# A hybrid DeltaNet, gating and Fourier step: first convolution tap on ScalarE, side work spread over the q, k, v loop, output weights' steps at other blocks

## The chip, the cores and the metric

The kernel runs on one core of one Trainium2 chip. The metric is the device time of one execution in microseconds (us); the time of a kernel is the median of several runs. The core has five engines that each work through a queue of their own in a fixed order: TensorE (PE, matrix products into PSUM; PEld is its loading of weights), VectorE (DVE), ScalarE (ACT), GpSimd (POOL) and SyncE (SP), which here only issues DMA transfers. An instruction waits in its queue on semaphores for what it needs from other engines, and everything behind it in that queue waits with it.

## The reference

One layer of a hybrid model is computed for 2048 sample tokens and 128 prompt tokens (2176 in all, width 1024), in float32. Cut to what matters here:

```
shift, scale, gate = split(silu(cond) @ w_ada + b_ada)
xn = rmsnorm(h) * (1 + scale) + shift
qkv, beta, dec, z_a, u_b, v_b, z_b, x_c, z_c, gates = split(xn @ w_in)
qkv = silu(conv3(qkv))                      # three taps along the tokens, per channel
q, k, v = split(qkv);  q, k = l2norm(q), l2norm(k)
beta = sigmoid(beta);  g = -exp(a_log) * softplus(dec + dt_bias)
o = gated delta rule of (q, k, v, g, beta), forward and backward in time, in chunks
o_a = rmsnorm(o) * silu(z_a)
o_b = spatial gating of (u_b, v_b) * silu(z_b)
o_c = Fourier mixing of x_c * silu(z_c)
merged = sum over n of sigmoid(gates_n) * (branch_n @ w_branch_n)
y = rmsnorm(h + gate * (merged @ w_out))
```

The outputs are y for both groups of tokens and the final states of the prompt's delta scans.

## The kernel before

**Numbers.** Each float32 operand of a large product is held as two float16 parts, hi and lo, after scaling by a power of two; a product is the three sums hi x hi, hi x lo, lo x hi. The tokens' parts are `xh` and `xl`, always in memory. The 1024 input rows are eight slices of 128 (`KT`), and the tokens five tiles (`TBS`): four of 512 and one of 128. A tile of one block of 128 columns is 24 products (`gemm_T`, L347, through the helper at L254).

**Weights.** A block of weights is loaded by SP (`read_w`) and then converted by the generator `converting` (L308) in steps: ScalarE sums the squares (L320); VectorE casts that sum (L268, tile `wscb`); TensorE multiplies it by a matrix of ones, a one-column product (L274, recorded under L254); VectorE makes scale and inverse (L282 to L284, L332); ScalarE writes the hi part (L335) and VectorE the lo part (L336). `weight_step` does one such step; `getw(n, ahead)` returns the next blocks and lets the conversions run `ahead` blocks further.

**Order.** A planner (list scheduling by priority, the order of writing unless said otherwise) fixes each engine's queue when the kernel is built. `tc.high_priority()` pulls instructions forward; `urgently()` (L247) does so for the conversion while the flag `urgent` is set, from L950 to L1012, that is over the q, k, v loop. `pace` spreads a generator over the work: `tick(us)` runs one weight step and as many steps of the generator as its quota of time units allows.

**The q, k, v loop** (L977 to L1005) goes over twelve blocks `ct`. Each tile's product is moved from PSUM to the row buffer `raw` by ScalarE (L990). Then come the three taps on VectorE (L996 to L998, into `cy`), the sigmoid on ScalarE (L1001) and the product on POOL (L1002) in four pieces, the store (L1003) and for eight of the blocks a sum of squares on ScalarE (L1005). `raw` and `cy` have two buffers each. PSUM gives these tiles six banks in turn (`ps_mm` and `ps_d`, three each).

Two generators run beside the loop. `token_sums` (L952) makes sums and differences of token quarters for a later product by Strassen's scheme, on VectorE and POOL, splits them on ScalarE (L969) and VectorE or POOL (L970), and stores them through SP; it has 72 steps. `decays` (L830) makes beta and the decays: a narrow product, a chain of small operations (L853 to L891), and then for each of 17 chunks a subtraction and a minimum of 128 x 1024 on VectorE (L929, L930), an exponential on ScalarE (L917) and a store on ScalarE's queue; it has some 40 steps.

**Later stages.** After the loop come the spatial gating branch, the Fourier branch and three merges, with the delta rule (`delta`, L1462) as filler through `pace`. The first merge (`merge(1, ...)`, L1865) and the second (`merge(2, ...)`, L2011) each go over eight blocks `db` of five tiles; the backward half of the scan runs there and ends each chunk with `finish` (L1421): the sum of both directions, a norm, four transposes (L1434), a product with silu(z_a) (L1436) and a store. `out_w` (L1827) converts the output weights in 48 steps, two column blocks at a time; the generator is advanced by the merges' `step`. `norm_step` (L1893) is the second merge's step; it also sums the squares of the third branch's weights (`early`, eight of them, L1903).

The last merge (L2214) goes over eight passes `n_` of eleven units `u`. It uses seven products of Strassen's scheme; `total` (L2076) adds two of them on VectorE. `gate_rows` (L1807) computes the gate vectors for the end there: eight loads of 512 KB, each followed by eight multiply-and-add operations of `ada_sum` (L484, L486).

Of the kernel before, what the change touches and what calls it, by code (L numbers as in the profile page):

```python
# [14 lines left out]
AF = mybir.ActivationFunctionType  # L15
# [5 lines left out]
P = 128  # L21
# [174 lines left out]
def hybrid_flow_kernel(ctx: ExitStack, tc: tile.TileContext, x_prompt, x_sample, state_delta, c, c_ctx, w_ada,  # L196
# [47 lines left out]

    newest, gated_, queued, urgent = [None], [None], [False], [False]

    def urgently():  # L247
        return tc.high_priority() if urgent[0] else ExitStack()

# [58 lines left out]
    def converting(w, st, nkt, cols=P, hi=None, lo=None, tag="w", bufs=5, nth=0):  # L308
# [9 lines left out]
        ss = sb(wp, [P, 1], "wss", bufs=4) if nth < KT else bsums[:, 3 + nth:4 + nth]  # L318
        with behind_gate(), urgently():
            w.squared = A.activation(w.lo, st, AF.Square, accum_out=ss)  # L320
        yield
        with urgently():
            sb16 = widened(ss, wp, "wsc")
        if wnext[0] < 11:
            yield
        with urgently():
            s, inv = scales(None, wp, "wsc", sb16)
            w.inv = sb(wp, [P, 1], "winv", bufs=10)
            if isx is None:
                w.own = inv  # L330
            else:
                V.tensor_mul(w.inv, inv, isx)  # L332
        yield
        with urgently():
            w.made = A.activation(w.hi, st, AF.Copy, scale=s)  # L335
            w.low = V.scalar_tensor_tensor(w.lo, st, s, w.hi, ALU.mult, ALU.subtract)  # L336

# [141 lines left out]
    def ada_sum(acc, st, ks, fresh=True):  # L479

        for g in range(2):
            for i, k in enumerate(ks):
                if i == 0 and fresh:
                    V.tensor_scalar(acc[:, g, :], st[:, i, :], scT[:, k, g:g + 1], None, ALU.mult)  # L484
                else:
                    V.scalar_tensor_tensor(acc[:, g, :], st[:, i, :], scT[:, k, g:g + 1], acc[:, g, :], ALU.mult, ALU.add)  # L486
# [462 lines left out]
    halves = slice(0, 4), slice(4, 8)  # L949
    urgent[0] = True  # L950

# [23 lines left out]
    flip = [0]  # L975
    pace.start(decays(), 1.2)
    for ct in range(12):  # L977
        w = getw(1, 2 if ct < 6 else min(4, 15 - ct))
        for half in range(1):
# [4 lines left out]
            for t0, tn in TBS:  # L984
# [6 lines left out]
                pace.tick(tn / 100)  # L991
                if tn == 512 and ct:
                    for _ in range(2):
                        next(beside, 0)
            y = sb(a1p, [P, LP - 2], "cy")
            V.tensor_scalar(y, raw[:, 0:LP - 2], convw(0, ct), None, ALU.mult)  # L996
            V.scalar_tensor_tensor(y, raw[:, 1:LP - 1], convw(1, ct), y, ALU.mult, ALU.add)  # L997
# [12 lines left out]
    for _ in beside:  # L1010
        pass
    urgent[0] = False  # L1012
    a1.close()
# [793 lines left out]
    def gate_rows():  # L1807
        for blk in range(4):
            cs = slice(2 * D + blk * 256, 2 * D + (blk + 1) * 256)
            acc = sb(wq_[0], [P, 512], "wt2").rearrange("p (g c) -> p g c", g=2)  # L1810
            for k0 in range(0, KT, 4):
                st = sb(wp, [P, 4, 256], "wst", bufs=2)
                SY.dma_start(st, w_ada_[k0 * P:(k0 + 4) * P, cs].rearrange("(k p) c -> p k c", p=P))
                yield 1
                ada_sum(acc, st, range(k0, k0 + 4), k0 == 0)
                yield 1
            gr = sb(ep, [P, 512], "st", bufs=3)[0:2, 0:256]
# [46 lines left out]
    s1_, inv_ = branch_scale(1, 20)  # L1864
    inv_ = merge(1, True, inv_, then=(2, 20), step=lambda db: next(weights_out, 0) if db else 0)  # L1865
    def finish_delta(db):
# [607 lines left out]
```

## Time and profile before

| | |
|---|---|
| median of three runs | 2210.57 us |
| lowest and highest | 2209.73 and 2214.68 us |
| profiled execution, its own time | 2209.05 us |
| profiled execution, span of its trace | 2207.3 us |
| TensorE, products | 2084.7 us, 94% |
| VectorE | 1445.0 us, 65% |
| ScalarE | 1096.3 us, 50% |
| GpSimd | 982.1 us, 44% |
| granted TensorE clock, mean | 0.979 |

The durations in the next parts are those of the profiled execution. The span is what the trace covers; the time of the execution has 1.75 us around it. Busy time of TensorE overlaps its own pipeline, so the distance between the starts of two products says more than the length of one. "Granted clock" is the share of full speed that TensorE got. In the tables of groups a line has the source line, engine and operation, what is written and read with shapes, the count, the busy time, the mean of one in ns, and the idle time of the engine before it with the instruction that ended it. In the lists of waits a line has who waited, for whom, the total in us, how often, and the longest.

### The profile page before, as it was taken

Reading aid. Unit: us, or ns where it says so; the run is one execution under the profiler, and the core shown is the slowest. Engines: PE = TensorE matmul, PEld = TensorE weight load, DVE = VectorE, ACT = ScalarE, POOL = GpSimd, SP = SyncE. Lnnn points to the kernel's source line nnn. Section 1 sums busy time; section 2 is a strip of 40 time slices with the busy share of each in tenths; the row PEclk is TensorE's granted clock in tenths of the full one; section 3 lists DMA queues with packets and bytes.
Section 4 is the critical chain, followed back from the end, with each engine's and each line's share of the span. In section 5 each row is a group of like instructions: output and inputs, shape, how many; then the busy total and the mean of one; then the engine's idle time right before and its main releaser. Section 6 shows DMA issues by size and latency. Waiting matters only on the chain.

```text
span 2207.3 us, 43369 instructions
## 1 busy us (share of the span) xinstructions
PE 2084.7 (94%) x16169; PEld 1194.0 (54%) x16169; DVE 1445.0 (65%) x3000; ACT 1096.3 (50%) x2513; POOL 982.1 (44%) x1178
## 2 busy tenths in 40 slices
PE   8998788999999999989899999989999999999998
PEld 4454334446555587768655655556565444444443
DVE  6668995439877777655667565766755276676445
ACT  5554563537556575444555454756665255322112
POOL 0346683323555745543323233445643245333454
PEclk9998899999999999999899999999999999999999
DMA  8525652327777574154566565786775685876762
GB/s 347 210 95 182 235 207 92 109 79 235 222 257 254 193 235 148 52 159 130 185 188 214 166 202 184 220 251 215 227 234 153 225 279 203 300 272 210 291 223 92
DMA packets 266211, 440.13 MB, mean 199 GB/s; under 512 B 47608, under 2 KB 148752, under 8 KB 262928
## 3 DMA queue, kind: packets, MB, share of 16 engines
q1 hardware_dynamic: 213488, 336.27, 47.3%
q0 software_dynamic: 12688, 57.04, 6.8%
q10 hardware_dynamic: 39824, 44.05, 5.8%
q8 instruction: 127, 2.08, 0.4%
q14 instruction: 84, 0.69, 0.1%
HBM read 276.61 MB, written 160.65 MB: 198 GB/s over the span
## 4 chain that ended last, share of the span: by engine, by line
PE 59%; DVE 15%; DMA 11%; issue 5%; ACT 4%; POOL 4%; SPq 1%; ACTq 0%; POOLq 0%; DVEq 0%
PE b L254 55%; PE b L183 3%; DMA wst<-in_w_blk_dram 2%; DMA st<-br 1%; DMA wo<-slot 1%; DMA sqk<-qk 1%; DVE xl L183 1%; POOL E L1167 1%; DVE pa L941 1%; PE b L1068 1%; DVE cy L997 1%; DVE st L970 1%; DMA ES<-ei 1%; DVE XB L1166 1%; DVE cy L998 1%
## 5 line engine op out<-in xcount | busy, mean ns | idle before, releaser
L254 PE MATMUL b<-xh,whi 128*128 128x512 f16 (+2 forms) x1792 | 604.8, 348 | 7.7 <-ACT sg L2128 3.4
L254 PE MATMUL b<-xl,whi 128*128 128x512 f16 (+2 forms) x1792 | 605.5, 348 | 0.0
L254 PE MATMUL b<-xh,wlo 128*128 128x512 f16 (+2 forms) x1792 | 602.9, 348 | 0.0
L254 PEld LDWEIGHTS <-whi 128*128 128x128 f16 x3872 | 350.5, 99 | 361.0 <-issue 52.3
L254 PEld LDWEIGHTS <-wlo 128*128 128x128 f16 x1936 | 190.6, 99 | 184.8 <-issue 18.3
L254 PE MATMUL b<-big,bhi 128*128 128x512 f16 (+1 forms) x960 | 251.6, 348 | 0.2
L254 PE MATMUL b<-big,blo 128*128 128x512 f16 (+1 forms) x480 | 163.0, 347 | 0.0
L254 PEld LDWEIGHTS <-xh 128*128 128x128 f16 x1512 | 118.4, 98 | 30.3 <-issue 1.0
L1167 POOL TENSOR_TENSOR E<-E,XB 128x31 f32<-128x31 f32 (+15 forms) x155 | 94.7, 611 | 84.6 <-DVE XB L1166 67.9
L254 PEld LDWEIGHTS <-bhi 128*128 128x128 f16 x960 | 87.1, 98 | 79.1 <-issue 3.8
L1002 POOL TENSOR_TENSOR cy<-cy,raw 128x545 f32<-128x545 f32 (+1 forms) x48 | 70.1, 1486 | 90.6 <-ACT raw L1001 90.6
L1240 POOL COPY T<-ES 32x256 f16<-32x256 f16 x68 | 31.7, 466 | 175.4 <-DMA ES<-ei 156.3
L254 PE MATMUL b<-whi,xh 128*128 128x128 f16 x544 | 92.8, 219 | 0.0
L254 PE MATMUL b<-wlo,xh 128*128 128x128 f16 x544 | 92.8, 219 | 0.0
L254 PE MATMUL b<-whi,xl 128*128 128x128 f16 x544 | 92.8, 219 | 0.0
L1347 POOL TENSOR_TENSOR skn<-skn,ed 128x512 f32<-128x512 f32 x34 | 36.5, 1075 | 112.9 <-DMA skn<-kv 112.9
L1166 DVE TENSOR_TENSOR XB<-XB,E 128x31 f32<-128x31 f32 (+15 forms) x155 | 55.4, 357 | 41.9 <-POOL E L1167 41.3
L254 PEld LDWEIGHTS <-xl 128*128 128x128 f16 x824 | 74.4, 98 | 15.0
L1790 POOL TENSOR_TENSOR mrow<-mrow,sg 128x512 f32<-128x512 f32 (+1 forms) x40 | 47.2, 1179 | 72.6 <-DVE sg L1789 54.8
L254 PEld LDWEIGHTS <-big 128*128 128x128 f16 x480 | 46.8, 98 | 59.4 <-DMA big<-pa 2.6
L254 PE MATMUL b<-xh,big 128*128 128x512 f16 x280 | 74.8, 379 | 1.6 <-DMA big<-pa 1.6
L960 POOL TENSOR_TENSOR sg<-xh,xl 128x512 f32<-128x512 f16 (+1 forms) x36 | 59.2, 1648 | 35.3 <-DVE st L970 14.9
(568 smaller groups left out, 4810.8 us busy)
## 6 DMA issues: line engine op xcount, KB each, us to landing
wst<-in_w_blk_dram SPq DMA_DIRECT2D x58, 512.0 KB, 4.3
pa<-pa POOLq DMA_DIRECT2D x16, 896.0 KB, 5.5
qkv<-cy POOLq DMA_DIRECT2D x12, 1089.0 KB, 4.9
st<-br SPq DMA_DIRECT2D x48, 256.0 KB, 3.6
big<-pa SPq DMA_DIRECT2D x12, 896.0 KB
dc<-dec SPq DMA_DIRECT2D x17, 512.0 KB, 5.8
kq<-qkv SPq DMA_DIRECT2D x34, 256.0 KB, 7.4
kv<-tok POOLq DMA_DIRECT2D x17, 512.0 KB, 5.2
```

The source lines that it names most:

```text
L183: self.last = f(*args, **kw)
L254: newest[0] = PE.matmul(out, l, r, start=start, stop=stop, skip_group_check=reopened)
L941: V.scalar_tensor_tensor(lo, src, s, hi, ALU.mult, ALU.subtract)
L960: on.tensor_tensor(f, xh[:, kk, ts], xl[:, kk, ts], ALU.add)
L970: (V if i % 2 else G).tensor_tensor(st[:, 1], f, st[:, 0], ALU.subtract)
L997: V.scalar_tensor_tensor(y, raw[:, 1:LP - 1], convw(1, ct), y, ALU.mult, ALU.add)
L1002: G.tensor_tensor(y[:, c0:c1], y[:, c0:c1], raw[:, 1 + c0:1 + c1], ALU.mult)
L1166: V.tensor_tensor(t3, X3[:, 0:k, k:k + 1].to_broadcast([P, k, n_]), E3[:, k:k + 1, k:32].to_broadcast([P, k, n_]), ALU.mult)
L1167: G.tensor_tensor(E3[:, 0:k, k:32], E3[:, 0:k, k:32], t3, ALU.subtract)
L1240: G.tensor_copy(T16[rows(a0, b), :, :, b], ES[0:32, :, 2 * a0 + b, :, wT])
L1347: G.tensor_tensor(h3(kn_), h3(kn_), bc(ed[:, d, t, :], P), ALU.mult)
L1790: G.tensor_tensor(mr, mr, sg, ALU.add)
```

## The change

- The flag `urgent` and `urgently()` go: the weight conversions of the q, k, v loop have no raised priority.
- `ada_sum` becomes a generator that goes over the rows first and over the two groups inside, with a step before each row's two operations; `gate_rows` passes its steps on, and the last merge advances it at every unit of passes 4 to 6 instead of every second.
- The decays' quota goes from 1.2 to 3.2 units per step; the token sums take one and two steps in turn per full tile from the first block on, instead of two per full tile from the second block on.
- The first tap is computed by ScalarE.
- The output weights' steps run in blocks 1 to 5 of the first merge (before: 1 to 7) and in blocks 4 to 6 of the second, two per tile (before: from block 0, one per tile); what is left runs after the second merge. The eight early sums run from block 2 of the second merge on, no longer after the output weights.

```diff
@@ converting
-        with behind_gate(), urgently():
+        with behind_gate():
             w.squared = A.activation(w.lo, st, AF.Square, accum_out=ss)
         yield
-        with urgently():
-            sb16 = widened(ss, wp, "wsc")
+        sb16 = widened(ss, wp, "wsc")
...
@@ ada_sum
-        for g in range(2):
-            for i, k in enumerate(ks):
+        for i, k in enumerate(ks):
+            yield 1
+            for g in range(2):
...
@@ the q, k, v loop
-    pace.start(decays(), 1.2)
+    pace.start(decays(), 3.2)
+    halfway = [0]
...
-                if tn == 512 and ct:
-                    for _ in range(2):
+                if tn == 512:
+                    halfway[0] ^= 1
+                    for _ in range(1 + halfway[0]):
                         next(beside, 0)
             y = sb(a1p, [P, LP - 2], "cy")
-            V.tensor_scalar(y, raw[:, 0:LP - 2], convw(0, ct), None, ALU.mult)
+            A.activation(y, raw[:, 0:LP - 2], AF.Copy, scale=convw(0, ct))
...
@@ gate_rows
-                yield 1
-                ada_sum(acc, st, range(k0, k0 + 4), k0 == 0)
-                yield 1
+                yield from ada_sum(acc, st, range(k0, k0 + 4), k0 == 0)
...
-    inv_ = merge(1, True, inv_, then=(2, 20), step=lambda db: next(weights_out, 0) if db else 0)
+    inv_ = merge(1, True, inv_, then=(2, 20), step=lambda db: next(weights_out, 0) if 0 < db < 6 else 0)
@@ norm_step
-        if next(weights_out, 0):
-            return
-        if early:
+        if db > 3 and db < KT - 1:
+            next(weights_out, 0)
+            next(weights_out, 0)
+        if 1 < db and early:
...
     inv_ = merge(2, False, inv_, finish_delta, then=(0, 17), step=norm_step)
+    for _ in weights_out:
+        pass
...
@@ the last merge
-            if 3 < n_ < 7 and u % 2 == 0:
+            if 3 < n_ < 7:
                 next(gates, 0)
```

More of the change, by code (lines that the diff above doesn't have):

```diff
@@ L243, in hybrid_flow_kernel @@
     G.memset(mhalf, -0.5)
-    newest, gated_, queued, urgent = [None], [None], [False], [False]
-    def urgently():
-        return tc.high_priority() if urgent[0] else ExitStack()
+    newest, gated_, queued = [None], [None], [False]
     def behind_gate():
@@ L318, in converting @@
         ss = sb(wp, [P, 1], "wss", bufs=4) if nth < KT else bsums[:, 3 + nth:4 + nth]
-        with behind_gate(), urgently():
+        with behind_gate():
             w.squared = A.activation(w.lo, st, AF.Square, accum_out=ss)
         yield
-        with urgently():
-            sb16 = widened(ss, wp, "wsc")
+        sb16 = widened(ss, wp, "wsc")
         if wnext[0] < 11:
             yield
[L326 to L332, printed above, removed]
+        s, inv = scales(None, wp, "wsc", sb16)
+        w.inv = sb(wp, [P, 1], "winv", bufs=10)
+        if isx is None:
+            w.own = inv
+        else:
+            V.tensor_mul(w.inv, inv, isx)
         yield
-        with urgently():
-            w.made = A.activation(w.hi, st, AF.Copy, scale=s)
-            w.low = V.scalar_tensor_tensor(w.lo, st, s, w.hi, ALU.mult, ALU.subtract)
+        w.made = A.activation(w.hi, st, AF.Copy, scale=s)
+        w.low = V.scalar_tensor_tensor(w.lo, st, s, w.hi, ALU.mult, ALU.subtract)
     def convert(st, nkt, *args, **kw):
@@ L949, in hybrid_flow_kernel @@
     halves = slice(0, 4), slice(4, 8)
-    urgent[0] = True
     def token_sums():
@@ L1011, in hybrid_flow_kernel @@
         pass
-    urgent[0] = False
     a1.close()
```

## The prediction

> **What bounds the kernel now.** I read the page first, then a table of windows, then the waits and the order of instructions inside the one stage that the table singles out. The page shows TensorE busy nearly all the time, with one long weak place:
>
> ```profile
> span 2207.3 us, 43369 instructions
> PE   8998788999999999989899999989999999999998
> DVE  6668995439877777655667565766755276676445
> PEclk9998899999999999999899999999999999999999
> ```
>
> A slice is 55.2 us. From slice 4 to slice 7 (166 to 386 us) TensorE falls to 7 and 8 and its granted clock to 0.8 and 0.9. In the first half of that stretch VectorE is at 8, 9, 9; right after it, while the same loop still runs, at 5, 4, 3. This is the convolution loop over the twelve blocks of q, k and v: its evictions (L990) run from 144.92 to 467.72 us. Windows with these borders (columns: the window, its length, busy time of PE, PEld, DVE, ACT and POOL, granted clock, DMA share, GB/s):
>
> ```profile
> 144.92:467.72 322.80, 281.15 (x1704) 138.69 (x1701) 231.89 (x252) 163.49 (x252) 178.78 (x165) 0.93 0.45 154
> 144.92:331.00 186.08, 151.38 (x999) 75.83 (x996) 171.10 (x168) 105.78 (x153) 134.67 (x104) 0.90 0.59 201
> 331.00:467.72 136.72, 129.77 (x707) 62.85 (x705) 60.80 (x84) 57.71 (x99) 44.11 (x61) 0.98 0.26 90
> ```
>
> TensorE idles 322.80 - 281.15 = 41.65 us, 34.7 of it in the first part. There VectorE is busy 171 of 186 us, in the second part 61 of 137. So the side work (token sums and decays) is packed into the first half, makes VectorE the bound there, and leaves it empty later. The list of waits of TensorE in this stage names the releaser:
>
> ```profile
> PE b L254 <- DVE wscb L268: 33.0, 6, 10.8
> PE b L254 <- DVE tok L877: 6.1, 1, 6.1
> ```
>
> Six times, 5.5 us each, TensorE's queue stood at the one-column product that sums a weight block's squares (`ones16` times `wscb`) because VectorE reached its tiny cast late. Everything behind that product in TensorE's queue waited too.
>
> An idle time costs more than its length. TensorE's order of time, in order, around the second wait:
>
> ```profile
> 159.67 0.38 PE L254 MATMUL b<-xh,wlo 128*128 128x512 f16 x1
> ...
> 168.52 0.38 PE L254 MATMUL b<-xl,whi 128*128 128x512 f16 x1
> 174.99 1.68 PE L254 MATMUL b<-tok,cst 128*128 128x68 f32 x6 [6.08 <-DVE tok L877]
> 176.45 0.63 PE L254 MATMUL b<-xh,wlo 128*128 128x512 f16 x1
> ...
> 180.72 0.63 PE L254 MATMUL b<-xh,whi 128*128 128x512 f16 x1
> ```
>
> The first two rows are the ends of 42 products: 8.85 us over 41 steps, 0.216 us each. After the idle 6.08 us, eleven products take 0.427 us each, half speed. Between the first and last eviction lie 47 full tiles and 12 short ones of 24 products: 47 x 24 x 0.216 = 243.6 us, and the short ones, a quarter as wide, 12 x 24 x 0.054 = 15.6 us. The decays' narrow products add this:
>
> ```profile
> L254 PE MATMUL b<-bdp,xh 128*128 128x32 f16 x136 | 7.3, 180 | 0.9 <-issue 0.9
> ```
>
> So TensorE alone would need 243.6 + 15.6 + 7.3 = 266.5 us, and the stage loses 322.8 - 266.5 = 56 us: 41.65 idle and 14.6 at half speed, that is 0.35 us more per idle us. These 56 us are all that leveling can return here.
>
> **The change part by part.** *Leveling.* The costliest groups of VectorE in and around the stage (140 to 485 us):
>
> ```profile
> L997 DVE SCALAR_TENSOR_TENSOR cy<-raw,pc,cy 128x2178 f32<-128x2178 f32 x12 | 32.5, 2708 | 0.1
> L998 DVE SCALAR_TENSOR_TENSOR cy<-raw,pc,cy 128x2178 f32<-128x2178 f32 x12 | 31.8, 2654 | 0.3
> L970 DVE TENSOR_TENSOR st<-sg,st 128x512 f16<-128x512 f32 x16 | 18.5, 1164 | 0.0
> L996 DVE TENSOR_SCALAR cy<-raw,pc 128x2178 f32<-128x2178 f32 x12 | 17.9, 1489 | 46.0 <-ACT raw L990 46.0
> L336 DVE SCALAR_TENSOR_TENSOR wlo<-wst,wsc,whi 128x1024 f16<-128x1024 f32 x11 | 16.6, 1517 | 3.4 <-ACT whi L335 3.3
> L929 DVE TENSOR_TENSOR dc<-dc,tok 128x1024 f32<-128x1024 f32 x8 | 13.9, 1742 | 0.6 <-DMA dc<-gamR 0.6
> L930 DVE TENSOR_TENSOR dc<-dc,cst 128x1024 f32<-128x1024 f32 x8 | 13.5, 1685 | 0.0
> L966 DVE TENSOR_TENSOR sg<-sg,sg 128x512 f32<-128x512 f32 x8 | 9.2, 1153 | 0.0
> L965 DVE TENSOR_TENSOR sg<-sg,sg 128x512 f32<-128x512 f32 x8 | 9.2, 1149 | 5.3 <-POOL sg L963 5.3
> L930 DVE TENSOR_TENSOR XB<-XB,cst 128x1024 f32<-128x1024 f32 x6 | 9.2, 1531 | 0.0
> L929 DVE TENSOR_TENSOR XB<-XB,tok 128x1024 f32<-128x1024 f32 x6 | 9.1, 1534 | 0.0
> L960 DVE TENSOR_TENSOR sg<-xh,xl 128x512 f32<-128x512 f16 x8 | 9.1, 1132 | 2.0 <-DMA sz<-sg 2.0
> ```
>
> Decays: 28 of their 34 wide operations cost 13.9 + 13.5 + 9.2 + 9.1 = 45.7 us, 1.63 each, so 55.5 us in all. The page's pacing units are us of TensorE at tn/100, 21.76 per block. Some 40 steps at 1.2 units end after 2.2 blocks; at 3.2 they end after 128 units, 5.9 blocks. Token sums: 72 steps, so far eight per block from block 1, done after block 9; now six per block from block 0, done with the last block. Their quoted rows give 18.5 + 9.2 + 9.2 + 9.1 = 46 us. The new demand on VectorE in the first six blocks is: convolution 6/12 x (32.5 + 31.8) = 32.2; decays 55.5; token sums 23; and of the rest (231.9 - 82.2 - 55.5 - 46 = 48: weight conversions, the decays' small chain, the short token block) some 28, because the small chain runs there. Sum 139 us. TensorE needs 6 x (96 x 0.216 + 24 x 0.054) + 7.3 = 139.5 us for the same six blocks. In the second six VectorE has about 75 us for 132. So leveling turns VectorE from a clear bound into a tie in the first half.
>
> A tie is not free on queues in fixed order: in the rows above VectorE itself waits 5.3 us for L963 on POOL and 3.3 for L335. I allow 10 us of idle TensorE for that, keep the 6.1 us wait of the decays' small chain (a serial chain; pacing moves its start, not its length) and 2 us of small ones: 18 x 1.35 = 24 us lost instead of 56. Gain 32 us. Bounds: 56 (nothing waits) and 0 (all the waits only move).
>
> *First tap on ScalarE.* It takes 17.9 us from VectorE (used above). On ScalarE nothing of that form is in the stage except the square over the same shape:
>
> ```profile
> L1005 ACT ACTIVATE raw<-cy 128x2178 f32<-128x2178 f32 x8 | 16.1, 2016 | 17.8 <-POOL cy L1002 17.8
> ...
> L1001 ACT ACT_TABLE_LOAD x5 | 6.4, 1283 | 0.5 <-ACT XB L917 0.4
> ```
>
> 12 x 2.016 = 24.2 us more on ScalarE: 163.5 + 24.2 = 188 of about 290 us, so it hides. What is queued behind the tap is the next block's evictions, up to 2 us late; PSUM holds six tiles of 5.2 us, so TensorE does not see it. If that cover were gone it would cost at most those 24 us. The decays' exponentials now fall between the sigmoids of six blocks, not three; if each of the 17 flushes reloaded the table twice, 34 x 1.28 = 44 us, ScalarE would be at 232 of 290, still covered. I take nothing, with 0 to 10 for the range.
>
> The Trainium skill speaks against this edit: "ScalarE: Activation LUTs", Rules for kernel authors, wants a plain multiplication on VectorE. The rows agree on the price of one (1.489 against 2.016 us); by the rule alone the sum would lose 6 us of engine time, but by the windows the dearer engine is the idle one.
>
> *Priority taken from the weight conversions.* No instruction goes or comes; the cast, the one-column product and the scaling stand where they are written, a tile or more behind each other, instead of at the first moment the planner thinks them ready. For TensorE a later product is a safer one; for the weights it is later readiness, and they are written one to two blocks (22 to 44 us) ahead. I take it as part of the 32, with the loss as a rival. SP's queue carries the weight loads, token stores and decay rows; all its entries stay, thinner in time.
>
> *Gate rows.* The sums (64 operations, two per step at every unit instead of eight at every second) start in the last merge's fifth pass:
>
> ```profile
> L486 DVE SCALAR_TENSOR_TENSOR wt<-wst,scT,wt x56: 462/472/1158, 1883.6 to 1994.9; 128x256 f32<-128x256 f32 x56
> ```
> ```profile
> PE b L254 <- DVE st L2076: 2.8, 1, 2.8
> ```
>
> Bursts of 8 x 0.47 = 3.8 us shrink to 0.95, and the 2.8 us wait (1860 to 2060 us) behind them should go: with half speed 2.8 x 1.35 = 3.8; I take 3. The loads are now issued only one step ahead of their first sum; a late one can hold VectorE, so -5 to +4.
>
> *Output weights.* In the merges the 48 steps now run in blocks 1 to 5 of the first (25) and 4 to 6 of the second merge (at two per tile), no longer in blocks 6, 7 and 0 to 2, where the scan's finishing begins. TensorE's waits there (1340 to 1600 us) and the weights' VectorE operations:
>
> ```profile
> PE b L1434 <- ACT o L1430: 4.5, 3, 2.9
> PE b L254 <- DVE o L1436: 2.1, 1, 2.1
> ```
> ```profile
> L941 DVE SCALAR_TENSOR_TENSOR slot<-osts,osc,slot x32: 734/750/1639, 1175.2 to 1560.6; 128x512 f16<-128x512 f32 x32
> ```
>
> 6.6 us of waits can shrink. Half of the 32 operations, 16 x 0.75 = 12 us of VectorE with as much on ScalarE, their stores on SP and POOL's differences, move into three blocks at double rate, beside the scan's last steps. I take 3 saved and 2 paid: +1, bounds -7 to +7.
>
> **Sum.** 32 + 3 + 1 = 36 us. The profiled execution took 2209.05 us (span 2207.3 and 1.75 around it): 2173. The median before is 2210.57, 1.5 above; so 2174.5.
>
> **The rivals.** *All waits go.* A decay operation takes 1212 ns at the least and 2175 at the most (minimum, median, maximum):
>
> ```profile
> L929 DVE TENSOR_TENSOR dc<-dc,tok x8: 1212/1918/2175, 196.8 to 294.8; 128x1024 f32<-128x1024 f32 x8
> ```
>
> POOL is busy 134.67 of the first 186 us, and I read the difference as waiting for it. With token sums thinned from eight to six steps per block, more of them run alone; at 1.21 the 34 take 41 us, not 55.5, VectorE needs 125 of 139.5 us and the tie is gone. Gain 52 + 4 + 2: about 2152. For it: the slack. Against: POOL's own work is unchanged and runs over the same blocks.
>
> The Trainium skill gives this rule ("SBUF - State Buffer", Who interferes with whom): VectorE with two SBUF inputs and GpSimd lock each other out of a shared port for whole instructions. The trace's 1212 and 2175 ns agree.
>
> *VectorE stays the bound.* The 139 us are an underestimate by 10% and the queue waits come on top: 25 us more idle and slow time, gain 5 to 15, about 2198.
>
> *Late conversions: slower.* With the priority gone, the chain cast, product, exponents, scaling of each of the 15 blocks (11 here, 4 for the next stage) stands behind decays and token sums in VectorE's queue at each link. At today's 5.5 us per wait (33.0/6), 15 waits cost 15 x 5.5 x 1.35 = 111 us, against 56 now: 2265. It is slower from about eight such waits on, 56/(5.5 x 1.35); ten give about 2230. For it: the longest wait was 10.8 us even with priority. Against: those waits fell where VectorE was full without a gap.
>
> *Nothing gained*: the waits move to other instructions, the total stays within 0.2%, 2206 to 2215.
>
> **How the numbers follow.** Forecast 2174.5 with 50% (its own range 2160 to 2190); all waits go 16%; VectorE stays the bound 16%; late conversions 12%; nothing 6%. A measurement of this kernel can tell about 0.2% (4.4 us) from no change. Faster: 50 + 16 + 16 = 82%; same 6%; slower 12%. The range from 2150 to 2207 holds the forecast, nearly all of the first two rivals and little else, about 80%.
>
> **What would show it.** Right: between first and last eviction 290 us or so, not 323; granted clock there above 0.96; VectorE near even over the loop; the wait on L268 below 10 us; the tap's group on ScalarE near 24 us. Wrong: a wait on L268 or on a weight (whi, wlo) of 20 us or more; evictions late behind the tap; VectorE full in blocks 0 to 5 and the decays' exponentials ending after block 7; a new wait in the merges near 1610 to 1740 us.

## The result and the profile after

The changed kernel takes **2185.28 us** (median of four runs, 2182.05 to 2187.63); the kernel before took 2212.62 us (four runs) on the same chip. The ratio is 0.9871, 95% interval 0.9844 to 0.9899. A second set of runs beside other kernels gave 2187.50 against 2209.39 us, ratio 0.9895 (0.9881 to 0.9909). So the change gains 22 to 27 us, where 36 were forecast.

The page of the profiled execution (2187.63 us) answers to the three lines shown of before:

```profile
span 2185.8 us, 43372 instructions
PE   8998989999999999999899999999999989999997
DVE  6669994448877776566656565766666477686345
PEclk9999999999999999999999999999999999999999
```

VectorE (DVE) still reads 9, 9, 9 in slices 4 to 6, and 4, 4, 4 right after, but the granted clock now reads 9 in every slice. The table of windows over the same loop, the convolution over q, k and v, from its first eviction (now 145.13) to its last (447.75), and its two parts (columns: window, length, busy PE, PEld, DVE, ACT, POOL, clock, DMA share, GB/s):

```profile
145.13:447.75 302.62, 277.40 (x1703) 136.65 (x1700) 215.91 (x242) 180.98 (x261) 172.90 (x165) 0.96 0.48 164
145.13:331.00 185.87, 165.02 (x1071) 81.38 (x1068) 166.58 (x169) 113.54 (x162) 132.68 (x114) 0.94 0.61 206
331.00:447.75 116.75, 112.39 (x634) 55.26 (x633) 49.33 (x73) 67.44 (x99) 40.22 (x51) 1.00 0.28 98
```

The loop is 20.2 us shorter (322.80 to 302.62). Idle time of TensorE fell from 41.65 to 25.22 us. Against the 266.5 us that TensorE alone needs, 36 us are lost: 25.2 idle, and the remaining 10.9 by the slow stretches behind idle times. In the first part VectorE is busy 166.6 of 186 us, hardly less than before, and in the second 49 of 117. The side work has **not** been spread. Windows of 20 us, same columns, show it sharper:

```profile
205.00:225.00 20.00, 20.00 (x113) 9.83 (x112) 19.95 (x18) 16.46 (x19) 11.11 (x11) 1.00 0.72 265
225.00:245.00 20.00, 20.00 (x113) 9.80 (x112) 20.00 (x14) 10.88 (x15) 15.84 (x10) 1.00 0.57 193
245.00:265.00 20.00, 15.63 (x85) 7.37 (x83) 20.00 (x20) 12.85 (x18) 9.31 (x8) 0.91 0.93 315
265.00:285.00 20.00, 14.66 (x87) 7.21 (x85) 20.00 (x16) 15.15 (x19) 19.35 (x11) 0.93 0.65 208
...
365.00:385.00 20.00, 19.93 (x112) 9.80 (x112) 7.31 (x9) 8.21 (x11) 5.32 (x4) 1.00 0.24 83
```

For 80 us VectorE has practically no gap (79.95 of 80 us busy); a hundred us later it is nearly two thirds empty. Yet from 205 to 245 us TensorE runs without a gap beside a full VectorE; before, it was busy 36.3 of these 40 us. What changed is what TensorE waits for (its waits in the loop: who, for whom, total us, times, longest):

```profile
PE b L251 <- DVE wlo L330: 10.2, 3, 5.3
PE b L251 <- DVE wscb L265: 4.4, 3, 2.0
PE b L891 <- DVE ed L883: 3.0, 1, 3.0
PE b L251 <- DVE tok L872: 2.6, 1, 2.6
```

The wait for the tiny cast of a weight block's squares (`wscb`, now L265) fell from 33.0 us in six to 4.4 in three. In its place stand 10.2 us for the weights themselves, their lo parts (`wlo`, now L330).

By stages, from the first and last starts of the evictions, of the first merge's first sigmoid and of the last merge's first copy (us; the first two rows are the two profiles just described, the third a second profile of the changed kernel, and the rest belongs to the experiments):

| kernel | loop | loop to first merge | merges | last merge to the end of the span |
|---|---|---|---|---|
| before | 322.8 | 612.6 | 702.3 | 424.7 |
| after | 302.7 | 615.5 | 694.8 | 427.7 |
| after_again | 304.9 | 617.8 | 695.0 | 424.6 |
| pace_back | 307.4 | 615.7 | 695.5 | 425.1 |
| tap_back | 314.2 | 613.5 | 693.5 | 425.8 |
| priority_back | 316.7 | 617.9 | 701.0 | 424.8 |
| product_late | 309.0 | 620.4 | 695.1 | 424.7 |
| prio_alone | 312.6 | 609.3 | 697.5 | 425.1 |
| outw_back | 303.5 | 617.3 | 699.5 | 424.4 |
| gates_back | 306.3 | 619.1 | 693.7 | 424.0 |

Two profiles of one kernel differ by 2 to 3 us in a stage, so smaller differences are not read. The gain is some 18 to 20 us in the loop and some 7 in the merges; the other two stages give nothing, and together they are 5 to 6 us longer than before in both profiles of the changed kernel. A table row is one profiled execution, which need not be a typical one: that of prio_alone (2191.26 us) was the fastest of its ten, and that of product_late (2195.31 us) the slowest of its four.

### The profile page after: what moved, and what is told of

Same layout as the page of the kernel before. It is cut to its first block, busy times and chain, and to the rows that moved or that the text cites. A ratio compares the mean times of both kernels' runs of the same rounds, so it can differ in the third digit from the quotient of the medians.

```text
span 2185.8 us, 43372 instructions
## 1 busy us (share of the span) xinstructions
PE 2081.8 (95%) x16169; PEld 1189.0 (54%) x16169; DVE 1439.0 (66%) x2988; ACT 1114.0 (51%) x2523; POOL 975.1 (45%) x1178
## 4 chain that ended last, share of the span: by engine, by line
PE 42%; DVE 10%; DMA 9%; ACT 4%; issue 4%; POOL 3%; SPq 1%; ACTq 0%; POOLq 0%; DVEq 0%
PE b L251 41%; DMA st<-br 2%; DMA wst<-in_w_blk_dram 1%; POOL E L1162 1%; DMA wo<-slot 1%; DVE slot L936 1%; DVE XB L1161 1%; DMA ei<-XB 1%; DMA tw<-slot 1%; DVE pa L936 1%; DVE big L1748 1%; DMA big<-pa 0%; ACT big L1747 0%; PE b L1063 0%; DVE o L1295 0%
## 5 line engine op out<-in xcount | busy, mean ns | idle before, releaser
L251 PE MATMUL b<-xh,whi 128*128 128x512 f16 (+2 forms) x1792 | 603.6, 347 | 10.2 <-DVE sg L1784 3.8
L251 PE MATMUL b<-xh,wlo 128*128 128x512 f16 (+2 forms) x1792 | 601.8, 347 | 10.2 <-DVE wlo L330 10.2
L251 PE MATMUL b<-xl,whi 128*128 128x512 f16 (+2 forms) x1792 | 604.0, 347 | 0.0
L251 PEld LDWEIGHTS <-whi 128*128 128x128 f16 x3872 | 348.7, 99 | 342.0 <-issue 34.8
L251 PEld LDWEIGHTS <-wlo 128*128 128x128 f16 x1936 | 189.9, 99 | 186.4 <-DVE wlo L330 11.9
L251 PE MATMUL b<-big,bhi 128*128 128x512 f16 (+1 forms) x960 | 252.8, 348 | 1.0 <-DVE big L1748 0.7
L251 PE MATMUL b<-big,blo 128*128 128x512 f16 (+1 forms) x480 | 162.9, 347 | 0.0
L251 PEld LDWEIGHTS <-xh 128*128 128x128 f16 x1512 | 119.9, 99 | 31.9 <-issue 3.2
L251 PEld LDWEIGHTS <-bhi 128*128 128x128 f16 x960 | 86.9, 98 | 79.0 <-issue 4.9
L251 PE MATMUL b<-wlo,xh 128*128 128x128 f16 x544 | 94.3, 221 | 0.0
L251 PE MATMUL b<-whi,xl 128*128 128x128 f16 x544 | 94.3, 221 | 0.0
L251 PE MATMUL b<-whi,xh 128*128 128x128 f16 x544 | 94.3, 221 | 0.0
L251 PEld LDWEIGHTS <-xl 128*128 128x128 f16 x824 | 74.9, 99 | 15.2 <-issue 0.8
L251 PEld LDWEIGHTS <-big 128*128 128x128 f16 x480 | 46.7, 98 | 60.2 <-DMA big<-pa 3.2
L251 PE MATMUL b<-xh,big 128*128 128x512 f16 x280 | 74.8, 379 | 2.2 <-DMA big<-pa 2.2
L330 DVE SCALAR_TENSOR_TENSOR wlo<-wst,wsc,whi 128x1024 f16<-128x1024 f32 x44 | 62.5, 1422 | 21.5 <-ACT whi L329 20.3
```

Source lines behind the costliest of these rows:

```text
L251: newest[0] = PE.matmul(out, l, r, start=start, stop=stop, skip_group_check=reopened)
```

## The experiments

Twelve kernels were run, in three groups that each shared their runs of the kernel before (medians 2209.67, 2209.26 and 2209.39 us). Two theories stood at the start. The prediction's: the gain is leveling, VectorE's side work thinned by its pacing. Its rival: the planner takes side work as soon as it is ready, so pacing in the order of writing moves little, and the gain is in the weight conversions' lost priority and in the tap.

### Pacing undone

```diff
-    pace.start(decays(), 3.2)
+    pace.start(decays(), 1.2)
...
-                if tn == 512:
-                    halfway[0] ^= 1
-                    for _ in range(1 + halfway[0]):
+                if tn == 512 and ct:
+                    for _ in range(2):
```

> Only the pacing is undone: the decays' quota is 1.2 again and the token sums take two steps per full tile from block 1. Theory A (the planner fills VectorE's free time with any ready side work, wherever it is written, so the pacing moves little): within 5 us of the changed kernel, 2181 to 2191 us, the loop still near 303 us. Theory B (the pacing levels VectorE's load, as the prediction had it): most of the 20 us that the loop gained is lost again, 2197 to 2207 us.

Measured: 2187.81 us (2185.76 to 2190.65), ratio 0.9888 (0.9864 to 0.9913); the changed kernel beside the same chip's runs of before stood at 0.9895. The pacing is worth nothing that can be told. VectorE's queue, as the program fixes it, says why. In order, t is a token sum's split on VectorE (L964 in the changed kernel), d a decay's minimum (L925), C a block's third tap (L994) and a dot a weight block's cast (L265); the first five dots come ahead of the loop, and the rest after the last C is left out:

```
before   .....tttttttd.dtdtdd C .tddd C ddtd.td C d.ddtdt C d.tt C .ttt.t C tttt. C .. C .... C . C  C  C
changed  .....ttttt.t C tddtddd C tddt.ddddtdt C .ddtddtd. C tt C ..tttttt.t C t. C .. C . C .. C . C . C
```

The kernel with the pacing undone, read in the same way from its trace (which may lack a record or two):

```
pace_back  .....tttttttd.ddtd C dtdtd C ddd.tdd C tdtddd.dt C .tt C .ttttttt.t C . C .. C . C .. C . C . C
```

In all three kernels all decays stand before the fifth third tap, and all token sums on VectorE before the seventh, though the changed kernel writes the last token sum in the twelfth block. The planner fills each engine with what is ready, and so pulls the side work forward from wherever it is written.

### First tap back on VectorE

```diff
-            A.activation(y, raw[:, 0:LP - 2], AF.Copy, scale=convw(0, ct))
+            V.tensor_scalar(y, raw[:, 0:LP - 2], convw(0, ct), None, ALU.mult)
```

> Only the first tap goes back to VectorE (12 operations of about 1.5 us, 18 us). Theory A (VectorE is the bound in the loop's first half, so what leaves it there is worth its length): about half of the taps fall into that half, so the loop is 8 to 14 us longer and the time 2193 to 2200 us. Theory B (leveled by the pacing, VectorE is no longer the bound): less than 5 us.

Measured: 2193.99 us (2192.71 to 2200.23), ratio 0.9922 (0.9895 to 0.9949). The tap is worth 6.5 to 9 us; in the loop it is 314.2 against 302.7 and 304.9. TensorE's waits of this kernel in the loop:

```profile
PE b L251 <- DVE wlo L330: 14.3, 2, 7.7
PE b L251 <- DVE wscb L265: 4.8, 1, 4.8
```

VectorE has 15 us more to do, and TensorE idles 33.2 us instead of 25.2. Which wait pays for the tap isn't shown: the lo parts come later here (14.3 us against 10.2), but in pace_back, which is no slower in total, they cost 15.8.

### Priority given back

```diff
-        sb16 = widened(ss, wp, "wsc")
+        with urgently():
+            sb16 = widened(ss, wp, "wsc")
...
+    urgent[0] = True
```

and the same around the squares, the exponents and the two parts, as in the kernel before.

> Only the raised priority of the weight conversions comes back. Theory A: the one-column product stands early in TensorE's queue again, its wait on the cast goes from 4 us back to 20 or more, and the time to 2193 to 2205 us. Rival: the priority does not matter, the wait stays below 10 us and the time within 4 us of 2185; then the waits moved to the conversions' last step are the same ones under another name.

Measured: 2205.57 us (2197.69 to 2209.43), ratio 0.9972 (0.9956 to 0.9988). This one part holds 18 to 20 of the 22 to 27 us, 12 to 14 of them in the loop. Another 6 lie in the merges (701.0 against 694.8 and 695.0), long after the stretch in which the flag is set; what makes them is not shown. The wait on the cast is back (L268 and L254 in this kernel are L265 and L251 of the changed one). First the largest row of TensorE's waits, then one of these waits in TensorE's order of time (start, length, what, and in brackets the idle time before it):

```profile
PE b L254 <- DVE wscb L268: 30.8, 4, 10.2
```
```profile
220.80 0.16 PE L254 MATMUL b<-wscb,ones 128*128 128x1 bf16 x1 [10.21 <-DVE wscb L268]
```

A product of 0.16 us held the whole of TensorE for 10.21.

### Priority alone taken from the kernel before

```diff
-    urgent[0] = True
```

> The kernel before with one thing changed: the weight conversions of the loop have no raised priority. Theory C (after the last runs: the priority is the main part, since with it the one-column product stands in TensorE's queue with no room behind the late cast): 2190 to 2199 us, the wait on the cast down from 33 us to below 15. Rival: the priority only pays together with the tap on ScalarE and the pacing, since with a full VectorE the wait moves to the conversion's last step: 2203 to 2212 us.

Measured: 2199.37 us (2191.26 to 2205.72), ratio 0.9962 (0.9946 to 0.9977): 8 to 10 us, just outside the first theory's range and better than the rival's. The waits of TensorE in its loop:

```profile
PE b L254 <- DVE wlo L336: 17.6, 4, 9.3
PE b L254 <- DVE wscb L268: 6.1, 1, 6.1
PE b L254 <- DVE tok L877: 4.9, 1, 4.9
```

The cast's 33.0 us fell to 6.1, but 17.6 us of waiting for lo parts came. So the rival saw something too: 17.6 of the 26.9 us that the cast no longer costs come back as late weights. In the changed kernel that new wait is 10.2 us, and the removal is worth 18 to 20, so the parts aren't additive. How the shares come about is not shown: this profile's own time was 2191.26 us, 8 below the median.

### The product alone written late

What is it in the priority that costs: the place of the one-column product in TensorE's queue, or VectorE's order? In this kernel everything has its priority back but that product.

```diff
+        total = bank(ps_x, [P, 1])
+        mm(total, ones16, sb16)
+        with urgently():
+            s, inv = exponents(total, sb(wp, [P, 4], "wsc"))
```

> The changed kernel with the raised priority given back to every step of the weight conversions but one: the one-column product that sums a block's squares stands where it is written. Two theories of why the raised priority cost some 20 us. Theory A, the place of the product in TensorE's queue: the priority put that product next to the cast that it waits for, so TensorE stood until VectorE, full at that time, had made the cast; with the product alone written later the waits on the cast (30.8 us in four with the priority given back) fall below 8 us and the time is 2185 to 2192. Theory B, VectorE's queue: the priority let scales and lo parts push the decays and taps back, so VectorE's order is what cost; then the time stays at 2198 to 2206 with the waits moved to other instructions, though the product stands late.

Measured: 2191.19 us (2187.87 to 2195.31), ratio 0.9913 (0.9897 to 0.9929), the wait on the cast 7.9 us. The first theory holds: of the 17 us (0.0077) between priority_back and after_again, this one edit returns 13 (0.0059). The last 4 lie within overlapping intervals. By the table 7.7 of these us are in the loop and 5.9 in the merges. Where the product stands, by the rows of cast and product from 145 to 340 us (count, shortest/median/longest ns, first and last start), first with the priority back:

```profile
L268 DVE CAST wscb<-wss x7: 138/143/159, 147.5 to 334.5; 128x1 bf16<-128x1 f32 x7
L254 PE MATMUL b<-wscb,ones x7: 163/163/167, 147.7 to 334.7; 128*128 128x1 bf16 x7
```

then with the product alone late:

```profile
L268 DVE CAST wscb<-wss x6: 138/144/156, 146.9 to 320.9; 128x1 bf16<-128x1 f32 x6
L254 PE MATMUL b<-wscb,ones x6: 163/167/167, 195.3 to 326.7; 128*128 128x1 bf16 x6
```

and in the changed kernel:

```profile
L265 DVE CAST wscb<-wss x7: 142/145/156, 147.7 to 333.2; 128x1 bf16<-128x1 f32 x7
L251 PE MATMUL b<-wscb,ones x7: 163/167/167, 199.8 to 333.4; 128*128 128x1 bf16 x7
```

With the priority, the product starts 0.2 us behind its cast, at the first as at the last: TensorE is there first, and each delay of VectorE is a stall. Without it the first product comes 48 to 52 us behind its cast. This room is used up on the way: in the changed kernel the seventh product, the last of these rows, stands 0.2 us behind its cast again (333.2 and 333.4 us), and the 4.4 us of waiting that are left fall on it and the two after it. By the order in TensorE's queue (number of the entry) the late product stands one whole block of 242 entries behind the last one, at the same places in product_late and in the changed kernel:

```
priority_back   1306  1852  2120  2360  2628  2840
product_late    1944  2186  2428  2670  2912
changed         1944  2186  2428  2670  2912
```

### Output weights and gate rows undone

```diff
-    ... step=lambda db: next(weights_out, 0) if 0 < db < 6 else 0)
+    ... step=lambda db: next(weights_out, 0) if db else 0)
...
-        if db > 3 and db < KT - 1:
-            next(weights_out, 0)
-            next(weights_out, 0)
-        if 1 < db and early:
+        if next(weights_out, 0):
+            return
+        if early:
```

> Only the output weights' steps go back to their old blocks. If keeping them away from the scan's outputs is what shortened the merges by 7.5 us (702.3 us from the first merge's first sigmoid to the last merge's first copy before, 694.8 after): 2190 to 2195 us, and waits of TensorE on L1425 and L1431 come back. Rival: that shortening comes from another order of the queues, not from this edit: within 3 us of 2185.

Measured: 2189.06 us (2183.45 to 2192.40), ratio 0.9914 (0.9892 to 0.9937). The total can't be told from that of the changed kernel. TensorE's waits between 1340 and 1600 us can: the first three rows of this kernel, then of the changed one.

```profile
PE b L1429 <- ACT o L1425: 4.4, 3, 2.4
PE b L251 <- DVE o L1431: 2.3, 1, 2.3
PE b L251 <- DVE R L1251: 1.8, 2, 1.2
```
```profile
PE b L1429 <- ACT o L1425: 1.1, 1, 1.1
PE b L251 <- DVE R L1251: 1.0, 1, 1.0
PE b L251 <- ACT Q L1233: 0.8, 1, 0.8
```

The two waits on the scan's finished outputs (`o`) are 6.7 us with the old places of the weights' steps and 1.1 with the new. The kernel before had 6.6 and prio_alone, also with the old places, 6.7. The merges went from 699.5 to 694.8 us. But their length doesn't follow these waits alone: priority_back has the new places and 0.4 us of such waits, and its merges take 701.0 us; prio_alone has the old places, and its merges take 697.5.

```diff
-        for i, k in enumerate(ks):
-            yield 1
-            for g in range(2):
+        for g in range(2):
+            for i, k in enumerate(ks):
...
-            if 3 < n_ < 7:
+            if 3 < n_ < 7 and u % 2 == 0:
```

> Only the gate rows' sums go back to eight per step at every second unit. The prediction gave this edit 3 us: 2187 to 2190 us with a wait on L2072 above the 3.8 us that the changed kernel has. Rival: nothing, within 2 us of 2185, since the last merge took 232 to 233 us from its first to its last copy in both kernels.

Measured: 2189.00 us (2187.71 to 2190.28), ratio 0.9917 (0.9899 to 0.9934). In the stage that it edits nothing changed: 424.0 us from the last merge's first copy, against 427.7 and 424.6. The wait that the prediction counted on, from 1860 to 2060 us, first with the old sums and then in the changed kernel:

```profile
PE b L251 <- DVE st L2073: 2.8, 1, 2.8
```
```profile
PE b L251 <- DVE st L2072: 2.8, 1, 2.8
```

It is the same in both and in before (L2076 there). The spreading of the sums has nothing to do with it.

### Side work held back by hand

If pacing in the order of writing doesn't spread the side work, an ordering that the planner must respect should. Here each block's side work may enter a queue only behind the third tap of the block before, and the decays' quota is 5.8 so that they last over the loop.

```diff
+    def held():
+        return tc.issue_after(tap[0].ins) if tap[0] is not None else ExitStack()
...
-                pace.tick(tn / 100)
+                weight_step()
+                with held():
+                    pace.steps(tn / 100)
+                    if tn == 512:
+                        halfway[0] ^= 1
+                        for _ in range(1 + halfway[0]):
+                            next(beside, 0)
```

> The changed kernel, with the side work truly held back: every VectorE, GpSimd and ScalarE step of the token sums and decays traced in a block is queued behind the third tap of the block before on that tap's engine, and the decays' quota is 5.8 units, so that they last to block 11. Theory A: VectorE is no longer full in any part of the loop (at most 85% in each half), the loop takes 275 to 288 us instead of 303, and the time is 2160 to 2172 us. Theory B: the loop is leveled already, so within 5 us of 2185, or slower where the decays end later than the next stage needs them.

Measured: 2193.18 us (2187.82 to 2194.44), ratio 0.9907 (0.988 to 0.9933), against 2160 to 2172 hoped for. The two halves of its loop, same columns as the windows above:

```profile
144.20:296.10 151.90, 149.98 (x1052) 76.59 (x1051) 109.10 (x114) 98.38 (x132) 80.24 (x76) 1.00 0.47 160
296.10:448.10 152.00, 124.58 (x659) 59.27 (x656) 100.10 (x128) 98.46 (x142) 78.28 (x90) 0.92 0.48 165
```

VectorE is now even (109 and 100 us), and in the first half TensorE idles under 2 us at full clock. But it idles 27 us in the second half, and the loop is as long as in the changed kernel (303.9 us). The wait there is again the cast (20.7 us in three), and followed back it leads to the squares on ScalarE and from there to the load of the weight block. SP issues these loads, and stores of the token sums stood in its queue, waiting for their data:

```profile
SPq L965 <- POOL st L964: 99.5, 11, 19.7
```

Whether they made the loads late was tried next. The token sums' stores were put on GpSimd's queue:

```diff
-                    SY.dma_start(sD[p_][:, i, :, k, :], st)
+                    G.dma_start(sD[p_][:, i, :, k, :], st)
```

> The held kernel (side work queued behind the block before, decays over eleven blocks) with the token sums' stores issued by GpSimd, not SyncE. Theory D (in the held kernel a token store waits up to 19.7 us on SyncE's queue for its data, and the weight load behind it starts late; that late load is what made the 20.7 us of waits on the cast in the loop's second half): the waits on the cast fall below 6 us, the loop to 276 to 288 us, the time to 2165 to 2175. Rival: the late cast has another cause (ScalarE's or VectorE's order), the loop stays near 304 us and the time at 2187 to 2194.

Measured: 2188.86 us (2184.08 to 2194.71), ratio 0.9917 (0.9893 to 0.9942), the wait on the cast 19.5 us. The stores were not the cause, or not alone: the decays' row loads now held SP's queue, up to 20.9 us at a time. So, with the stores left on GpSimd's queue, the rows were loaded one chunk ahead, not three:

```diff
-        ready = [rows_of(t) for t in range(3)]
+        ready = [rows_of(t) for t in range(1)]
...
-            if t + 3 < NCH:
-                ready.append(rows_of(t + 3))
+            if t + 1 < NCH:
+                ready.append(rows_of(t + 1))
```

> The kernel with the side work held behind each block's third tap and the stores of the token sums on GpSimd's queue (2188.86 us, weight casts waited for 19.5 us in its second half), with one edit: the decay rows are loaded one chunk ahead instead of three. Theory A: the weight loads stand in SP's queue behind row loads that wait for a buffer, 19 to 21 us at a time; then a shorter lead frees SP, the waits on the casts fall below 8 us and the time is 2165 to 2178. Theory B: the casts are late on VectorE itself, behind wide operations that holding pushed into the second half; then SP's queue empties and the waits on the casts stay at 15 to 20 us, 2183 to 2192. A lead of one chunk may itself hold VectorE for a load of about 2 us per chunk, under 5 us in all.

Measured: 2195.73 us (2191.97 to 2200.84), ratio 0.9935 (0.992 to 0.995). In its second half (299.7 to 454.9 us) VectorE, ScalarE and SP's queue waited for this, a list each:

```profile
DVE wscb L265 <- ACT wlo L317: 13.0, 4, 4.7
DVE wscb L265 <- ACT v4lo L317: 9.7, 3, 5.2
```
```profile
ACT v4lo L317 <- DMA wst<-in_w_blk_dram: 13.0, 4, 4.6
ACT wlo L317 <- DMA wst<-in_w_blk_dram: 10.5, 4, 3.4
```
```profile
SPq L293 <- DVE v4lo L330: 50.5, 4, 18.8
SPq L908 <- DMA dec<-E: 21.0, 1, 21.0
SPq L908 <- DMA dec<-XB: 19.6, 1, 19.6
```

Neither theory is borne out. VectorE stands idle 22.7 us before these casts, so it isn't too full for them; it waits for the squares on ScalarE, and these wait for the load (`wst`), 23.5 us. The edit didn't free SP: the row loads still hold its queue 20 us at a time for a buffer. But they are not what makes the weights late. The weight loads (L293) wait for a buffer themselves: `wst` has two, and VectorE's lo part (L330) of an earlier block is the last reader of the one that a load writes. The chain that ends in the longest of TensorE's waits in this half (start, length, what, and in brackets the idle time before it):

```profile
307.49 1.27 DVE L330 SCALAR_TENSOR_TENSOR wlo<-wst,wsc,whi 128x1024 f16<-128x1024 f32 x1
308.79 0.33 SPq L293 DMA_DIRECT2D wst<-in_w_blk_dram  x1
314.81 1.06 ACT L317 ACTIVATE wlo<-wst 128x1024 f16<-128x1024 f32 x1 [3.33 <-DMA wst<-in_w_blk_dram]
315.99 0.16 DVE L265 CAST wscb<-wss 128x1 bf16<-128x1 f32 x1 [2.58 <-ACT wlo L317]
316.20 0.16 PE L251 MATMUL b<-wscb,ones 128*128 128x1 bf16 x1 [7.33 <-DVE wscb L265]
```

The load is issued 0.03 us after the end of the lo part. So are eight of the nine weight loads of this half (the ninth 0.58 us after), and all nine in held_58 and in the kernel with the stores moved. In this half of these three kernels, then, the other steps in SP's queue held the weight loads back by 0.58 us at most. The second of the three waits (7.14 us) has the same chain; before the third (5.58 us) the load had been issued 19 us ahead of the squares, which came late on ScalarE behind side work and evictions. Last, the decays alone were held, with the same quota of 5.8 and the rows one chunk ahead, and with the stores on SP:

```diff
-                pace.tick(tn / 100)
+                weight_step()
+                with held():
+                    pace.steps(tn / 100)
                 if tn == 512:
                     halfway[0] ^= 1
```

> The changed kernel with the decays alone held behind each block's third tap (quota 5.8, rows one chunk ahead), the token sums as in the changed kernel. Theory A: what TensorE lacks is VectorE free of bursts in the first six blocks, and the decays are the larger part (some 55 of 101 us); with them thinned the idle time of the loop falls to 12 us or less and the time is 2172 to 2182. Theory B: whatever side work stays free is pulled into the gap that holding leaves, here the token sums, so VectorE is as full as before in the first half and the time is 2184 to 2192.

Measured: 2197.11 us (2194.21 to 2199.25), ratio 0.9935 (0.9921 to 0.9949), slower than both theories said; its loop is 318.1 us, with 14.4 us of waiting for the casts. Beside the casts there is one idle time of 11.0 us for which the profile names no releaser. Holding the decays, with their rows one chunk ahead and the token sums left free, is worse than holding nothing; how much of that is the rows' shorter lead wasn't separated. What an even VectorE would be worth with the weight loads in time stays **open**. By the rows above, a DMA queue of their own would not bring these loads forward; a third buffer for them, or an earlier place for the lo part, wasn't tried.

### The changed kernel again

> The changed kernel unaltered, run beside the next three so that all four share one chip and one set of runs of the kernel before. It was 2185.28 us against 2212.62. If the kernels with one part undone lie where their differences to it put them (pacing undone 2187.81, gate rows 2189.0, output weights 2189.06), it should come out at 2185 to 2189; if it comes out at 2188 or more, the two or three us that were read from those differences belong to the chip and not to the parts.

Measured: 2187.50 us (2185.92 to 2188.95), ratio 0.9895 (0.9881 to 0.9909). It lies within 2 us of pacing, gate rows and output weights undone, so no difference in the total is claimed for any of these three. The priority stands clear of it, and of the product alone written late (their intervals don't meet). The tap's runs do too (the lowest without the change of the tap is 2192.71, the highest here 2188.95), though the intervals of the ratios overlap.

## Why the prediction was right, and where it was wrong

The direction, the place (the q, k, v loop) and the waiting product on the cast were right; the time, 2185.28 us, lies in the likeliest case's own range, 11 us above the forecast. The path to it was another: the sum rested on 32 us from leveling, which didn't happen. That two other edits, for which the sum had no terms of their own, brought 18 to 20 us in the same loop is in part luck.

**Leveling failed as a mechanism.** The step "So leveling turns VectorE from a clear bound into a tie in the first half" is wrong. It took the order of writing for the order of the queues. VectorE is full from 205 to 285 us, as the quoted windows show, and the pacing undone costs nothing that can be told. The term of 32 us came out as 18 to 20, from two other sources.

**Priority** was the larger. The prediction saw its mechanism ("For TensorE a later product is a safer one; for the weights it is later readiness") and gave it no term of its own. Both halves of that sentence were measured: the cast's wait went from 33.0 to 4.4 us, and 10.2 us of waiting for `wlo` came. Most of it (13 of 17 us) is the product's place in TensorE's queue, by the kernel that changes nothing else; 5.9 of the 13 stand in the merges, which the prediction didn't connect with this edit and the runs don't explain. The rival of late conversions is the same mechanism with a higher price: it charged 15 waits at 5.5 us, and the runs show three of 3.4.

**The tap** was the smaller source, and right in its cost (12 operations on ScalarE, at 2104 ns instead of the 2016 taken):

```profile
L993 DVE SCALAR_TENSOR_TENSOR cy<-raw,pc,cy 128x2178 f32<-128x2178 f32 x12 | 31.6, 2634 | 18.0 <-ACT cy L992 18.0
L992 ACT ACTIVATE cy<-raw,pc 128x2178 f32<-128x2178 f32 x12 | 25.3, 2104 | 0.2
```

These are two groups of the changed kernel between 140 and 465 us. The 25.3 us on ScalarE hide from TensorE, which waits 0.9 us for an eviction in the loop; VectorE is 16.0 us less busy (231.89 to 215.91). The Trainium skill's rule for this ("ScalarE: Activation LUTs", Rules for kernel authors), a plain multiplication on VectorE, would have lost 6.5 to 9 us here, by tap_back.

**Gate rows:** the step "the 2.8 us wait (1860 to 2060 us) behind them should go" was wrong; it stayed at 2.8. The wait was put down to a neighbour in time. Of the 3 us nothing can be told.

**Output weights:** "I take 3 saved and 2 paid" was too low on the first: 5.5 us of waits went (6.6 to 1.1). The merges are 7.3 to 7.5 us shorter than before, and outw_back loses 4.5 to 4.7 of them again. But priority_back, with these places kept, loses 6.0 to 6.2, so the 7 us can't be put down to this edit alone, and its total can't be told from nothing.

**The rivals.** *All waits go* rested on decay operations that run alone more often. The changed kernel's row for them (shortest, median, longest):

```profile
L924 DVE TENSOR_TENSOR dc<-dc,tok x8: 1211/2165/2176, 196.1 to 289.7; 128x1024 f32<-128x1024 f32 x8
```

The median rose from 1918 to 2165 ns. The sums weren't thinned out, and of the 34 wide decay operations 16 took under 1.4 us, against 19 before. That GpSimd is what lengthens these operations was not tested. *VectorE stays the bound* was right for the first half, and wrong in that the time still fell: what cost TensorE most in the kernels with the priority was not that VectorE was full, but that a product stood right behind an instruction of VectorE's.

Of the signs named beforehand, the wait on the cast came out below 10 us (4.4) and the wait on a weight below 20 (10.2); the loop took 302.62 us instead of about 290, and the granted clock reached 0.96 and not more. Of the signs of being wrong, late evictions did not come (0.9 us of waiting). "VectorE full in blocks 0 to 5" came; the decays' exponentials ended at 296.8 us, earlier than before (308.6), when pacing should have ended them later.

## What to carry to other kernels

A raised priority puts a whole chain early in every queue that it touches. For a small step on the bounding engine that waits for a busy one, look at the time between the start of its input and its own, and at how often the engine idles there: a 0.16 us product that was queued next to its input started 0.2 us behind it and cost up to 10.21 us at a time; queued one block later, it cost 4.4 to 7.9 us in a whole loop. Where a planner fills queues with what is ready, check a spreading by the order in the queues before counting on it; and when a load is late, look at what ended just before it was issued: a long wait elsewhere in the same DMA queue (19.7 us) need not be the cause, when the load goes out 0.03 us after its buffer comes free.

## What had not been expected of the hardware

TensorE ran 40 us without a gap (205 to 245 us) beside a VectorE that was busy 19.95 and 20.00 of 20 us: the busy share of an engine does not tell the loss by itself. In the 40 us after that, with VectorE as full, TensorE waited 4.37 and 5.34 us for lo parts. And single steps held SP's queue for 19.7 to 21.0 us, stores and loads alike; taking one kind out of the queue left the waits on the weights' casts at 19.5 to 20.7 us. The weight loads behind the longest of these waits went out the moment their buffer came free.
